# Last output projections tile by tile with kept weights and other normalisations, first loads by two queues, and rotations in steps

## The chip, the cores and the metric

The kernel runs on one core of a Trainium2 chip. The metric is the device time of one execution in microseconds (us); lower is better. The engines are named as in the profile: PE does matmuls and transposes, DVE and ACT elementwise work, POOL a few elementwise steps and DMA issues, SP DMA issues.

## The reference, cut to what matters

```python
# x: (1, 512, 2048) float32; layer 0 is attention, layer 1 retention
def attention_mixer(h, w_in, q_gain, k_gain, w_out, cos, sin):
    q, k, v, g = split(h @ w_in)            # 2048 | 512 | 512 | 2048 columns
    q = apply_rope(rms_norm(q, q_gain), cos, sin) * (128 ** -0.5)
    k = apply_rope(rms_norm(k, k_gain), cos, sin)
    o = softmax(q @ k.T) @ v                # 16 heads, 4 kv heads, not causal
    return (o * silu(g)) @ w_out
def retention_mixer(h, w_in, decay_exp, w_out, cos, sin):
    q, k, v, g = split(h @ w_in)            # 2048 | 2048 | 4096 | 4096 columns
    q, k = apply_rope(q, cos, sin), apply_rope(k, cos, sin) * (256 ** -0.5)
    o = head_group_norm(fwd(q, k, v) + bwd(q, k, v))   # 8 heads, two directions
    return (o * silu(g)) @ w_out
x = layer_norm(ALPHA * x + attention_mixer(x, ...), ln_gain[0], ln_bias[0])
x = layer_norm(ALPHA * x + retention_mixer(x, ...), ln_gain[1], ln_bias[1])
```

## The kernel before

All is float32, and the kernel keeps that precision: each factor is split into a rounded part and a remainder, and a product of two matrices is three matmuls into the same PSUM bank (`mm3`, L218 to L222: both rounded parts L220, the weights' remainder L221, the features' remainder L222). The split (`split`, L103) is a cast on ACT (L104) and a subtraction on DVE (L105). Weights come as chunks of 128 x 1024 (512 KB), loaded by `raw_load` on SP's queue (L112) and split into `whi` and `wlo`; the list `order` says which chunk comes when, `next_chunk` splits two chunks ahead (AHEAD) and loads three more ahead (FETCH). `whi` and `wlo` have three buffers each, raw chunks nine; 32 larger buffers (`x4`) hold features, forms of features, row sums and the heads' operands. There are eight PSUM banks.

PE runs its instructions in the order in which the program issues them (`manual_schedule`); the other engines are put in order by the tile scheduler, and each runs its own list strictly in turn. A `Stream` is a generator of matmul work that is pumped by microseconds between other work.

The input projections are `Block`s of two column blocks of 512 each. A block is made in seven products (Strassen's way, so seven where eight would be needed) of four chunks each; the sums of weights that this takes are made by accumulating DMAs on POOL's queue (`onto`, L116) and by DVE, the sums of features ("forms") by DVE at the places that FORMS lists. `evacuate` combines the products, and `deliver_1` or `deliver_2` hands on a row tile of 128 rows of one column block: v and the gate are stored to DRAM, q and k are first rotated. `turn_soon` puts a rotation off by one to six chunks and then issues it as a whole: `rotate` (attention: square on ACT L528, gain L529, sums L533, six rotation steps L537 to L539, then a power on POOL L414; keys are also scaled L570) or `rope_2` (retention). Three chunks later `put` transposes the result (L431) and stores it.

The attention layer is then computed in four groups, the retention in eight heads, each pumping the output projection of the group or head before it (`Plain`, eight chunks, four column blocks by four row tiles). The last projection of either layer (`out_proj_last`) has no group or head behind it: it goes through all eight chunks for row tiles 0 and 1 and then a second time, loaded and split again, for tiles 2 and 3; after each sum DVE takes its statistics (L402).

After attention `norm_1` normalises two tiles and `turn_1` transposes them into the features of the retention, in pieces of 128 columns, while PE goes on with the second pass and then with the retention's input projection. After retention `norm_2` normalises two tiles at a time: centring and finishing on DVE (L926, L931) for two or three of the four column blocks, the others on ACT (L939) and POOL (L940, L941), and stores them on SP (L922).

At the start, `start` loads the first chunk in two halves and the first features in four pieces, all on SP's queue, then whole chunks.

## Time and profile before

| | us |
|---|---|
| median of 3 runs | 2203.59 (2201.79 to 2204.91) |
| profiled execution, its own time | 2198.51 |
| its span | 2196.6 |
| PE busy in the span | 2142.0 |
| DVE busy | 1586.9 |
| ACT busy | 1043.4 |
| POOL busy | 341.5 |
| mean clock granted to PE | 0.992 of full speed |

The profiled execution is 5.1 us below the median of the runs, and 1.9 us of it lie outside the span. A row of a timeline gives the start, the duration, engine, line, operation and tiles, and in brackets how long the engine had been idle and what it waited for. Matmuls are pipelined, so their durations overlap, and the pace is read from start to start. A granted clock below 1.00 in a window means that PE ran slowly there.

### The profile page before, as it was taken

How to read it: one execution, taken by the hardware profiler on the slowest of the kernel's cores; microseconds unless marked ns; L12 is line 12 of the kernel's file. 1: busy time of each engine (PE TensorE's matmuls, PEld its weight loads, DVE VectorE, ACT ScalarE, POOL GpSimd, SP SyncE). 2: the span in 40 equal slices, each digit the busy share in tenths (PEclk: the TensorE clock that was granted, in tenths of full speed). 3: DMA queues.
4: the chain of work that ended last, by engine and by line, in shares of the span. 5: the costliest groups of instructions: out<-in, count | busy, mean ns of one | idle time of the engine just before them, and what ended most of it. 6: DMA issues, size and time to landing. Idle time of an engine off the chain costs nothing.

```text
span 2196.6 us, 26556 instructions
## 1 busy us (share of the span) xinstructions
PE 2142.0 (98%) x9888; PEld 1767.6 (80%) x9888; DVE 1586.9 (72%) x2189; ACT 1043.4 (48%) x1365; POOL 341.5 (16%) x391
## 2 busy tenths in 40 slices
PE   8999999999999999999999999999999999999994
PEld 6778788888888778878888888888888888888883
DVE  6766978887778986767786676657677666666668
ACT  5545446754455654444444444444465333333332
POOL 0322434000000121211212111111111000000004
PEclk9999999999999999999999999999999999999997
DMA  9976666543215688686777558566667433343342
GB/s 337 211 195 133 169 173 148 184 177 106 95 60 171 207 189 220 163 244 177 176 198 210 132 142 213 155 130 183 178 162 262 160 117 107 122 135 125 101 139 77
DMA packets 111600, 361.42 MB, mean 165 GB/s; under 512 B 13680, under 2 KB 17008, under 8 KB 111472
## 3 DMA queue, kind: packets, MB, share of 16 engines
q1 hardware_dynamic: 76272, 235.99, 32.4%
q0 software_dynamic: 35200, 123.75, 25.7%
q8 instruction: 77, 1.26, 0.2%
q14 instruction: 51, 0.42, 0.1%
HBM read 311.45 MB, written 48.23 MB: 164 GB/s over the span
## 4 chain that ended last, share of the span: by engine, by line
PE 82%; DVE 7%; DMA 4%; issue 3%; POOL 2%; ACT 1%; SPq 0%; POOLq 0%; ACTq 0%; DVEq 0%
PE acc L221 23%; PE acc L222 23%; PE acc L220 23%; PE tr L431 3%; DVE wlo L105 3%; DMA raw<-in_wa_in_dram 2%; PE o L220 2%; PE o L222 2%; PE o L221 2%; DMA raw<-in_wr_in_dram 2%; PE s L220 1%; PE s L222 1%; PE s L221 1%; ACT whi L104 1%; DVE f L105 1%
## 5 line engine op out<-in xcount | busy, mean ns | idle before, releaser
L105 DVE TENSOR_TENSOR wlo<-raw,whi 128x1024 fp32r<-128x1024 f32 (+1 forms) x589 | 716.9, 1221 | 362.2 <-ACT whi L104 355.4
L104 ACT CAST whi<-raw 128x1024 fp32r<-128x1024 f32 (+1 forms) x589 | 618.8, 1052 | 744.2 <-PE acc L222 651.4
L220 PE MATMUL acc<-whi,f 128*128 128x512 f32 x1904 | 750.5, 394 | 9.3 <-ACT f L104 4.5
L221 PE MATMUL acc<-wlo,f 128*128 128x512 f32 x1904 | 745.0, 391 | 6.6 <-DVE wlo L105 6.4
L222 PE MATMUL acc<-whi,f 128*128 128x512 f32 x1904 | 743.8, 391 | 0.7 <-DVE f L105 0.7
L221 PEld LDWEIGHTS acc<-wlo,f 128*128 128x128 f32 x1904 | 358.7, 188 | 85.3 <-DVE wlo L105 13.4
L220 PEld LDWEIGHTS acc<-whi,f 128*128 128x128 f32 x1904 | 358.6, 188 | 83.9 <-ACT whi L104 5.2
L222 PEld LDWEIGHTS acc<-whi,f 128*128 128x128 f32 x1904 | 358.3, 188 | 76.7 <-DVE f L105 1.6
L221 PE MATMUL acc<-wlo,ogh 128*128 128x512 f32 x768 | 301.3, 392 | 11.5 <-DVE wlo L105 11.5
L220 PE MATMUL acc<-whi,ogh 128*128 128x512 f32 x768 | 306.0, 398 | 0.5 <-ACT p L604 0.5
L222 PE MATMUL acc<-whi,ogl 128*128 128x512 f32 x768 | 301.0, 392 | 0.0
L221 PEld LDWEIGHTS acc<-wlo,ogh 128*128 128x128 f32 x768 | 145.5, 189 | 40.5 <-DVE wlo L105 12.7
L222 PEld LDWEIGHTS acc<-whi,ogl 128*128 128x128 f32 x768 | 145.2, 189 | 31.1
L220 PEld LDWEIGHTS acc<-whi,ogh 128*128 128x128 f32 x768 | 145.1, 189 | 28.7 <-ACT p L604 0.9
L116 POOL DMA_DIRECT2D raw<-in_wr_in_dram x104 | 91.7, 882 | 384.0 <-DVE wlo L105 246.7
L365 DVE TENSOR_TENSOR y<-acc,y 128x512 f32<-128x512 f32 x176 | 115.6, 684 | 18.7 <-PE acc L222 18.7
L414 POOL TENSOR_TENSOR rstd<-rs_e,neg_half 128x1 f32<-128x1 f32 x40 | 23.8, 597 | 674.4 <-DVE rs_e L413 674.4
L154 DVE TENSOR_TENSOR raw<-raw,raw 128x1024 f32<-128x1024 f32 x52 | 63.5, 1223 | 35.9 <-DMA raw<-in_wr_in_dram 30.9
L152 DVE TENSOR_TENSOR raw<-raw,raw 128x1024 f32<-128x1024 f32 x68 | 82.1, 1218 | 0.8
L328 ACT COPY t<-acc 128x512 f32<-128x512 f32 x102 | 59.0, 587 | 41.9 <-PE acc L222 38.0
L867 ACT ACTIVATE o<-o,nmr,rstd 128x512 f32<-128x512 f32 x32 | 24.9, 779 | 93.4 <-DVE nmr L425 93.4
L604 ACT ACTIVATE p<-s,nmax,q_rs 128x512 f32<-128x512 f32 x64 | 50.0, 781 | 30.6 <-DVE nmax L602 28.2
(159 smaller groups left out, 2098.8 us busy)
## 6 DMA issues: line engine op xcount, KB each, us to landing
raw<-in_wr_in_dram SPq DMA_DIRECT2D x152, 512.0 KB, 4.8
raw<-in_wr_in_dram POOLq DMA_DIRECT2D x104, 512.0 KB, 6.1
raw<-in_wr_o_dram SPq DMA_DIRECT2D x72, 512.0 KB, 3.5
raw<-in_wa_in_dram SPq DMA_DIRECT2D x67, 512.0 KB, 5.1
raw<-in_wa_in_dram POOLq DMA_DIRECT2D x48, 512.0 KB, 6.4
raw<-in_wa_o_dram SPq DMA_DIRECT2D x40, 512.0 KB, 3.5
qkD<-qkT POOLq DMA_DIRECT2D x32, 256.0 KB, 4.4
vDr<-t POOLq DMA_DIRECT2D x32, 256.0 KB, 5.4
```

The costliest lines, as they stand in the source:

```text
L104: nc.scalar.copy(hi, src)
L105: nc.vector.tensor_sub(lo, src, hi.bitcast(F32))
L116: nc.gpsimd.dma_start(out=x, in_=src, accum_op=ALU.add)
L152: nc.vector.tensor_add(v, v, g[3, c])
L154: nc.vector.tensor_add(v, v, g[2, c])
L220: nc.tensor.matmul(ps, sh, mh, start=start, stop=False, skip_group_check=go_on)
L221: nc.tensor.matmul(ps, sh, ml, start=False, stop=False, skip_group_check=go_on)
L222: nc.tensor.matmul(ps, sl, mh, start=False, stop=stop, skip_group_check=go_on)
L328: nc.scalar.copy(keep[p, t], bk[CHAIN[p]][t])
L365: nc.vector.tensor_add(y, ps, y)
L431: nc.tensor.transpose(out=b[:, tcols(i)], in_=src[:, tcols(i)], identity=ident)
L604: nc.scalar.activation(pt, sb, AF.Exp, scale=rs, bias=nmax, accum_out=self.sm[:, h:h + 1])
```

## The change

It has five parts. (1) `out_proj_last` works tile by tile with kept weights: chunks of a `Plain` from column block `keep` on are split into `x4` buffers (`wkh`, `wkl`) and stay. The attention's last projection does column blocks 0 and 1 for all tiles as before (A_KEEP = 2) and then blocks 2 and 3 for one tile after the other; the retention's keeps all (R_KEEP = 0). The second pass over the chunks goes. (2) The norms are made per tile. `norm_1` keeps DVE's statistics. `norm_2` has its sums from the adding instruction itself (`accum_out`), its squares from ACT, and centres and finishes on DVE alone; `turn_1` takes two tiles together in pieces of 256. (3) `start` loads the first two chunks in halves on SP's queue and the first features on ACT's, and splits both chunks by halves. (4) Attention's column blocks are paired so that each block has one to rotate, and rotations are generators of which one step runs per chunk. (5) The forms 3, 7 and 4 are made in this order over the products 5, 3 and 7, and form 7 overwrites x11.

```diff
-A_COLS = ((("v", 0), ("g", 0)), (("g", 1), ("k", 0)), (("q", 0), ("q", 1)), (("q", 2), ("g", 2)), (("q", 3), ("g", 3)))
+A_COLS = ((("v", 0), ("k", 0)),) + tuple((("g", i), ("q", i)) for i in range(4))
...
+A_KEEP, R_KEEP = 2, 0
...
+            self.w, self.got, self.keep = w, {}, keep
...
-        hi, lo = [wp.tile([P, CH], F32R, tag=n, name=nm(n)) for n in ("whi", "wlo")]
+        if isinstance(blk, Plain) and p >= blk.keep:
+            hi, lo = x4("wkh"), x4("wkl")
+        else:
+            hi, lo = [wp.tile([P, CH], F32R, tag=n, name=nm(n)) for n in ("whi", "wlo")]
...
             elif n == 7:
-                nc.vector.scalar_tensor_tensor(out=x22, in0=x11, scalar=-1.0, in1=x22,
+                nc.vector.scalar_tensor_tensor(out=x11, in0=x11, scalar=-1.0, in1=x22,
                                                op0=ALU.mult, op1=ALU.subtract)
-            split(*self.new_form(n, i), {1: x11, 2: x12, 5: x21, 6: x11, 4: x22, 3: x12, 7: x22}[n])
+            split(*self.new_form(n, i), {1: x11, 2: x12, 5: x21, 6: x11, 4: x22, 3: x12, 7: x11}[n])
...
+        while steps:
+            if next(steps[0], steps) is not steps:
+                break
+            steps.pop(0)
...
-        soon((1, 4, 3, 6)[t], fn, src)
+        steps.append(gen(t, src))
...
+            if last and t not in self.st:
+                self.st[t] = small("ln_st", 24)
+            if last and t not in self.quick:
+                nc.vector.scalar_tensor_tensor(out=y, in0=y, scalar=scale, in1=ps, op0=ALU.mult, op1=ALU.add,
+                                               accum_out=self.st[t][:, c:c + 1])
...
+            if last and t in self.quick:
+                nc.vector.bn_stats(self.st[t][:, 6 * c:6 * c + 6], y)
+        def out_proj(self, og, scale, cols=(0, 1, 2, 3), last=False):
...
+            for c in cols:
...
+                    self.add(t, c, banks[t], scale, last)
+        def mean_rstd(self, t):
+            if t in self.quick:
+                return mean_rstd(self.st[t])
+            mu, neg, sq, rstd = small("k_rs", 4)[:, 0:1], small("nmr"), small("sm", 4), small("rstd")
+            nc.vector.tensor_reduce(out=mu, in_=self.st[t][:, :4], axis=AX.X, op=ALU.add)
+            nc.vector.tensor_scalar_mul(neg, mu, -1.0 / D)
+            nc.vector.tensor_scalar_mul(mu, mu, 1.0 / D)
+            for c in range(4):
+                nc.scalar.activation(temp("sq"), self.y[t, c], AF.Square, bias=neg, accum_out=sq[:, c:c + 1])
+            nc.vector.tensor_reduce(out=neg, in_=sq, axis=AX.X, op=ALU.add)
+            rsqrt(rstd, neg, 1.0 / D, LN_EPS)
+            return mu, rstd
...
+        def out_proj_last(self, og, keep):
+            yield from self.out_proj(og, 1.0, range(keep), True)
+            ws = {}
+            for t in range(NT):
+                for c in range(keep, 4):
+                    b = bank()
+                    for k in range(4):
+                        if t == 0 and k % 2 == 0:
+                            ws[c, k // 2] = next_chunk()
+                        mm3(b, og(k, t), ws[c, k // 2][k % 2], k == 0, k == 3)
+                        yield MM3
+                    self.add(t, c, b, 1.0, True)
+                self.rows.append(t)
...
+    a_out = [Plain(a["wa_o"][g], A_KEEP if g == GROUPS - 1 else 4) for g in range(GROUPS)]
+    r_out = [Plain(a["wr_o"][h], R_KEEP if h == R_HEADS - 1 else 4) for h in range(R_HEADS)]
...
-        outs[-1].add(1)
...
-    FORMS = (((1, 2, 1), (6, 0)), ((1, 2, 3), (6, 1)), ((0, 5, 0), (4, 0)), ((0, 5, 1), (4, 1)),
-             ((0, 5, 2), (3, 0)), ((0, 5, 3), (3, 1)), ((0, 6, 0), (7, 0)), ((0, 6, 1), (7, 1)))
+    FORMS = (((1, 2, 1), (6, 0)), ((1, 2, 3), (6, 1)), ((0, 5, 1), (3, 0)), ((0, 5, 3), (3, 1)),
+             ((0, 3, 0), (7, 0)), ((0, 3, 2), (7, 1)), ((0, 7, 0), (4, 0)), ((0, 7, 2), (4, 1)))
...
+        nc.scalar.copy(small("nmax"), neg_half[:, 0:1])
+        features(0, slice(1, 2))
+        features(0, slice(2, 4))
+        features(1, slice(0, 4))
+        chunks = []
+        for c in range(2):
+            raw = rp.tile([P, CH], F32, tag="raw", name=nm("raw"))
+            for j in range(2):
+                nc.sync.dma_start(out=half(raw, j), in_=half(blk.quarter(11, c), j))
+                if c == j == 0:
+                    features(0, slice(0, 1), nc.sync)
+            chunks.append([raw] + [wp.tile([P, CH], F32R, tag=n, name=nm(n)) for n in ("whi", "wlo")])
+        fetched[0] = 2
         fetch_to(4)
+        for c, (raw, hi, lo) in enumerate(chunks):
+            for j in range(2):
+                k = 2 * c + j
+                if k < 3:
+                    split_features(0, slice(k, k + 1) if k < 2 else slice(2, 4))
+                split(half(hi, j), half(lo, j), half(raw, j))
+            ready.append([(half(hi, j), half(lo, j)) for j in range(2)])
+        split_features(1, slice(0, 2))
+        split_features(1, slice(2, 4))
...
-    def rotate(t, qk, src):
...
+    def rotate(t, qk, src, g, put):
...
+        yield
         ss = small("r_ss", 4)
         nc.vector.tensor_reduce(out=ss, in_=v4(sq), axis=AX.X, op=ALU.add)
+        if qk == 0:
+            rs = q_rs[:, g, t]
+        else:
+            rs = small("k_rs", 4)
+        rsqrt(rs, ss, 1.0 / P, RMS_EPS)
+        yield
+        dst = temp("r_dst")
...
         for i in range(2):
             nc.vector.tensor_tensor(out=tv[:, :, :, i], in0=xv[:, :, :, 1 - i], in1=sb, op=ALU.mult)
+            if i:
+                yield
             nc.vector.tensor_tensor(out=dv[:, :, :, i], in0=xv[:, :, :, i], in1=cb, op=ALU.mult)
+            if not i:
+                yield
             nc.vector.tensor_tensor(out=dv[:, :, :, i], in0=dv[:, :, :, i], in1=tv[:, :, :, i],
                                     op=ALU.subtract if i == 0 else ALU.add)
-        return dst, ss
+        yield
+        if qk:
+            nc.vector.tensor_tensor(out=v4(dst), in0=v4(dst), in1=rs.unsqueeze(2).broadcast_to([P, 4, P]), op=ALU.mult)
+        soon(3, put, dst)
 
...
-                soon(3, put, m)
-            turn_soon(turn, t, src, own)
+            turn_soon(lambda t, src: rotate(t, 0 if kind == "q" else 1, src, g, put), t, src, own)
...
-    total = Sum()
+    total = Sum(range(NT))
...
-    def turn_1(t, c):
...
+    def turn_1(r, m):
+        b = bank("tr")
+        kh, i = m // 4, m // 2 % 2
+        for k in (2 * m, 2 * m + 1):
+            for t in range(2):
+                nc.tensor.transpose(out=b[:, tcols(k % 2 * 2 + t)],
+                                    in_=total.y[2 * r + t, k // 4][:, tcols(k % 4)], identity=ident)
+        for k in (2 * m, 2 * m + 1):
+            o = 256 * (k % 2)
+            f = x2.quarter(r, kh, i)[:, k % 4]
+            if k % 2:
+                nc.vector.tensor_scalar(f, b[:, o:o + 256], lnt[:, 0, k:k + 1], lnt[:, 1, k:k + 1],
+                                        op0=ALU.mult, op1=ALU.add)
             else:
...
+                nc.scalar.activation(f, b[:, o:o + 256], AF.Identity, scale=lnt[:, 0, k:k + 1], bias=lnt[:, 1, k:k + 1])
+        if r == 0 and m % 2:
+            x2.form(1 + kh, i)
...
+            yield
...
+        soon(3, put, m1)
...
-            turn_soon(lambda src: soon(3, put, rope_2(t, src)), t, src, own)
...
     def norm_2(t):
-        mu, rstd = mean_rstd(total.st[t])
...
+        mu, rstd = total.mean_rstd(t)
+        z = [half(m, j) for m in (x4("z", F32), x4("z", F32)) for j in range(2)] if t > 1 else [temp("z") for _ in range(4)]
+        for c in range(4):
...
+            nc.vector.scalar_tensor_tensor(out=z[c], in0=y, scalar=mu, in1=lnp[0][c], op0=ALU.subtract, op1=ALU.mult)
+        for c in range(4):
             y = total.y[t, c]
...
+            nc.vector.scalar_tensor_tensor(out=y, in0=z[c], scalar=rstd, in1=lnp[1][c], op0=ALU.mult, op1=ALU.add)
+            nc.sync.dma_start(out=out[t, :, c * 512:c * 512 + 512], in_=y)
...
-    work = Stream(total.out_proj_last(groups[-1].out), in_stream(r_in, x2, ev2, 1))
...
+    work = Stream(total.out_proj_last(groups[-1].out, A_KEEP), in_stream(r_in, x2, ev2, 1))
+    for r in range(2):
+        for t in (2 * r, 2 * r + 1):
+            work.until(lambda: t in total.rows)
+            norm_1(t)
+        work.pump(13.0 if r else 5.0)
+        for m in (0, 1, 4, 5, 2, 3, 6, 7) if r else range(8):
+            turn_1(r, m)
+            work.pump(2.2 if r else 0.8)
+            if r and m in (5, 7):
+                x2.form(5, m // 2 % 2)
...
-    work = Stream(total.out_proj_last(heads[-1].out))
-    work.pump(20.0)
+    work = Stream(total.out_proj_last(heads[-1].out, R_KEEP))
+    work.pump(5.0)
     ln_params()
...
+    for t in range(NT):
+        work.until(lambda: t in total.rows)
+        norm_2(t)
```

At the end, DVE's rows between the norms of tiles 0 and 1 (`nmr`, L926, L931) and the sums of tiles 2 and 3 in the kernel before; `wlo` are remainders of weights, `y` the row sums:

```order
L926 SCALAR_TENSOR_TENSOR y_13876<-y_13876,mv_17556,ln_gain_17506 128x512
L931 SCALAR_TENSOR_TENSOR y_13872<-y_13872,rstd_17536,ln_bias_17510 128x512
L425 TENSOR_SCALAR nmr_17563<-mv_17556,rstd_17558 128x1
L931 SCALAR_TENSOR_TENSOR y_13876<-y_13876,rstd_17558,ln_bias_17510 128x512
L926 SCALAR_TENSOR_TENSOR y_13876<-y_13876,mv_17556,ln_gain_17506 128x512
L105 TENSOR_TENSOR wlo_17591<-raw_17474,whi_17590 128x1024
L931 SCALAR_TENSOR_TENSOR y_13876<-y_13876,rstd_17558,ln_bias_17510 128x512
L365 TENSOR_TENSOR y_13880<-acc_17530,y_13880 128x512
L365 TENSOR_TENSOR y_13884<-acc_17578,y_13884 128x512
L402 BN_STATS ln_st_17607<-y_13880 128x6
```

and in the changed kernel DVE's rows up to the first step of the first norm (L978); `wkl` are the kept remainders, `ln_st` the sums that the adds give, and six of the eight `wkl` stand in the rows above these:

```order
L106 TENSOR_TENSOR wkl_17317<-raw_17269,wkh_17316 128x1024
L379 SCALAR_TENSOR_TENSOR y_13782,ln_st_17281<-y_13782,acc_17256 128x512
L106 TENSOR_TENSOR wkl_17327<-raw_17284,wkh_17326 128x1024
L379 SCALAR_TENSOR_TENSOR y_13782,ln_st_17281<-y_13782,acc_17283 128x512
L379 SCALAR_TENSOR_TENSOR y_13784,ln_st_17281<-y_13784,acc_17315 128x512
L379 SCALAR_TENSOR_TENSOR y_13784,ln_st_17281<-y_13784,acc_17337 128x512
L410 TENSOR_REDUCE k_rs_17355<-ln_st_17281 128x1
L411 TENSOR_SCALAR nmr_17356<-k_rs_17355 128x1
L412 TENSOR_SCALAR k_rs_17355<-k_rs_17355 128x1
L379 SCALAR_TENSOR_TENSOR y_13786,ln_st_17399<-y_13786,acc_17351 128x512
L978 SCALAR_TENSOR_TENSOR z_17374<-y_13782,k_rs_17355,ln_gain_17306 128x512
```

The splits of the weights stood between the norms' steps; now all are ahead of the first norm, and one tile's adds (L379) are followed by its norm.

From attention to retention, DVE's rows before, around the chunk at which PE waits 2.83 us (`wlo_6447`); `f` are splits of forms, L748 the turning of rows:

```order
L105 TENSOR_TENSOR f_6380<-xf_6374,f_6379 128x4x128
L748 TENSOR_SCALAR xf_6353<-tr_6429,lnt 128x128 x2
L748 TENSOR_SCALAR xf_6400<-tr_6395,lnt 128x128 x2
L402 BN_STATS ln_st_6333<-y_3756 128x6
L105 TENSOR_TENSOR f_6359<-xf_6353,f_6358 128x4x128
L365 TENSOR_TENSOR y_3760<-acc_6362,y_3760 128x512
L105 TENSOR_TENSOR f_6406<-xf_6400,f_6405 128x4x128
L402 BN_STATS ln_st_6336<-y_3760 128x6
L105 TENSOR_TENSOR wlo_6447<-raw_6300,whi_6446 128x1024
L748 TENSOR_SCALAR xf_6374<-tr_6458,lnt 128x128 x2
L748 TENSOR_SCALAR xf_6400<-tr_6475,lnt 128x128 x2
```

and now around the first chunk of the retention's projection that is split behind the last tile's norm (`wlo_6527`, the fourth chunk of that projection); L386 are statistics, L782 the norm, L800 the turning:

```order
L386 BN_STATS ln_st_6153<-y_3768 128x6
L447 BN_AGGR mv_6504<-ln_st_6153 128x2
L442 TENSOR_SCALAR rs_e_6507<-mv_6504 128x1
L454 TENSOR_SCALAR nmr_6510<-mv_6504,rstd_6506 128x1
L106 TENSOR_TENSOR f_6449<-xf_6435,f_6448 128x1024
L782 TENSOR_SCALAR y_3766<-y_3766,mv_6504,rstd_6506 128x512
L800 TENSOR_SCALAR xf_6460<-tr_6455,lnt 128x256
L800 TENSOR_SCALAR xf_6460<-tr_6476,lnt 128x256
L782 TENSOR_SCALAR y_3766<-y_3766,mv_6504,rstd_6506 128x512
L106 TENSOR_TENSOR wlo_6527<-raw_6256,whi_6526 128x1024
L106 TENSOR_TENSOR f_6484<-xf_6460,f_6483 128x1024
L106 TENSOR_TENSOR wlo_6545<-raw_6268,whi_6544 128x1024
```

There is no split of a weight among the sums of the last tile now; the next one stands behind that tile's statistics and norm (L447 to L782).

At the start, ACT's rows before:

```order
L104 ACT_TABLE_LOAD
L104 CAST whi_96<-raw_95 128x512
L104 CAST f_99<-xf_98 128x256 x2
L104 CAST whi_96<-raw_95 128x512
L104 CAST f_99<-xf_98 128x256 x2
L104 CAST whi_123<-raw_119 128x1024
L104 CAST f_127<-xf_121 128x1024
L104 CAST whi_141<-raw_131 128x1024
L104 CAST whi_165<-raw_133 128x1024
```

and now, with DMA issues of the features among them:

```order
L515 DMA xf_95<-in_xq_dram 128x256
L520 ACT_TABLE_LOAD
L520 COPY nmax_101<-neg_half 128x1
L515 DMA xf_95<-in_xq_dram 128x512
L515 DMA xf_96<-in_xq_dram 128x1024
L105 CAST f_97<-xf_95 128x256
L105 CAST whi_110<-raw_106 128x512
L105 CAST f_97<-xf_95 128x256
L105 CAST whi_110<-raw_106 128x512
L105 CAST f_97<-xf_95 128x512
L105 CAST whi_115<-raw_112 128x512 x2
L105 CAST f_99<-xf_96 128x512 x2
```

ACT issues three loads, loads its table early by a copy of one element, and casts the second chunk (`whi_115`) in two halves, the features' last two pieces as one.

More of the change, by code (lines that the diff above doesn't have):

```diff
@@ L483, in start, with features, split_features @@
         blk = order[0][0]
[L484 to L500 removed]
+        xf, fs = [x1.quarter(0, 0, i) for i in range(2)], [x1.new_form(1, i) for i in range(2)]
+        def features(i, ks, eng=nc.scalar):
+            eng.dma_start(out=xf[i][:, ks], in_=a["xq"][0, 0, i][:, ks])
+        def split_features(i, ks):
+            split(*[m[:, ks] for m in fs[i]], xf[i][:, ks])
+        nc.scalar.copy(small("nmax"), neg_half[:, 0:1])
[11 more added lines that the diff above has]
+        fetched[0] = 2
+        fetch_to(4)
+        for c, (raw, hi, lo) in enumerate(chunks):
[7 more added lines that the diff above has]
+        split_features(1, slice(2, 4))
     def tables():
@@ L579, in load_kv @@
         def load_kv(self):
+            assert all(("k", 0, t) in stored for t in range(NT))
             self.k, self.v = x4("k"), x4("v")
@@ L833, in load_qk @@
         def load_qk(self):
+            assert all((self.h, t) in stored for t in range(NT))
             self.qk = split_load(qkD[self.h])
@@ L918, in norm_2 @@
     def norm_2(t):
-        mu, rstd = mean_rstd(total.st[t])
-        def store(c):
-            nc.sync.dma_start(out=out[t, :, c * 512:c * 512 + 512], in_=total.y[t, c])
-        def centre(c):
+        mu, rstd = total.mean_rstd(t)
+        z = [half(m, j) for m in (x4("z", F32), x4("z", F32)) for j in range(2)] if t > 1 else [temp("z") for _ in range(4)]
+        for c in range(4):
             y = total.y[t, c]
-            return nc.vector.scalar_tensor_tensor(out=y, in0=y, scalar=mu, in1=lnp[0][c],
-                                                  op0=ALU.subtract, op1=ALU.mult)
@@ L929, in finish @@
-        def finish(c):
+            nc.vector.scalar_tensor_tensor(out=z[c], in0=y, scalar=mu, in1=lnp[0][c], op0=ALU.subtract, op1=ALU.mult)
+        for c in range(4):
             y = total.y[t, c]
-            nc.vector.scalar_tensor_tensor(out=y, in0=y, scalar=rstd, in1=lnp[1][c], op0=ALU.mult, op1=ALU.add)
-            store(c)
-        own = 2 if t < NT - 1 else 3
-        centre(0)
-        scale, shift = scale_shift(mu, rstd)
-        for c in range(own, 4):
-            y = total.y[t, c]
-            nc.scalar.activation(y, y, AF.Identity, scale=scale, bias=shift)
-            nc.gpsimd.tensor_mul(y, y, lnp[0][c])
-            nc.gpsimd.tensor_add(y, y, lnp[1][c])
-            store(c)
@@ L943, in norm_2 @@
-        finish(0)
-        for c in range(1, own):
-            tc.keep_in_program_order(centre(c))
-            finish(c)
-    ev2 = spill(deliver_2)
-    work = Stream(total.out_proj_last(groups[-1].out), in_stream(r_in, x2, ev2, 1))
-    work.until(lambda: 0 in total.rows)
-    norm_1(0)
-    norm_1(1)
-    work.pump(4.0)
-    for t in range(2):
-        for c in (0, 1, 2, 3):
-            turn_1(t, c)
-            work.pump(1.2)
-    work.until(lambda: 2 in total.rows)
-    norm_1(2)
-    norm_1(3)
```

112 lines of the change are left out of this document (20 added, 92 removed).

## The prediction

> **What bounds the kernel now.** I read the page first, then the waits of PE stretch by stretch, then the timelines around the longest waits.
>
> ```profile
> PE 2142.0 (98%) x9888; PEld 1767.6 (80%) x9888; DVE 1586.9 (72%) x2189; ACT 1043.4 (48%) x1365; POOL 341.5 (16%) x391
> 0.00:30.00 30.00, 22.49 (x74) 16.46 (x74) 14.74 (x18) 15.59 (x20) 0.20 (x4) 0.89 0.93 356
> 50.00:300.00 250.00, 243.32 (x1085) 198.00 (x1084) 192.15 (x263) 130.18 (x154) 88.07 (x71) 1.00 0.72 171
> 660.00:860.00 200.00, 193.29 (x904) 158.62 (x904) 166.63 (x237) 110.53 (x149) 32.81 (x43) 0.99 0.70 192
> 860.00:1300.00 440.00, 436.85 (x1942) 358.69 (x1941) 306.83 (x354) 203.00 (x228) 77.30 (x108) 1.00 0.72 189
> 2150.00:2197.00 47.00, 18.29 (x70) 14.01 (x68) 37.35 (x45) 8.11 (x10) 24.06 (x17) 0.73 0.24 89
> ```
>
> The first line is the page's busy shares; the others are the windows view: the stretch, its length, then busy time of PE, weight loads, DVE, ACT and POOL, the granted clock, DMA share, GB/s. PE is busy for 2142 of 2196.6 us, and both kernels issue the same matmuls and transposes. So the change can only take back the 55 us in which PE is not busy, and stretches at a low clock, and nothing in the middle of a stage at full pace. The idle time lies at five places: 7.5 us in the first 30, 6.7 between 50 and 300 (attention's in-projection), 6.7 between 660 and 860 (attention's last projection and the step to retention), 3.2 up to 1300 (retention's in-projection), and 28.7 in the last 47. The changed parts lie at the same five places.
>
> **The end: the last output projection and the last norms.** PE first, then DVE and POOL.
>
> ```profile
> 2151.68 0.39 PE L222 MATMUL acc<-whi,ogl 128*128 128x512 f32 x1
> 2151.91 0.39 PE L220 MATMUL acc<-whi,ogh 128*128 128x512 f32 x1
> 2160.78 0.80 PE L221 MATMUL acc<-wlo,ogh 128*128 128x512 f32 x1 [8.48 <-DVE wlo L105]
> 2165.18 0.40 PE L222 MATMUL acc<-whi,ogl 128*128 128x512 f32 x1
> ...
> 2176.55 0.39 PE L222 MATMUL acc<-whi,ogl 128*128 128x512 f32 x1
> 2158.44 2.28 DVE L105 TENSOR_TENSOR wlo<-raw,whi 128x1024 fp32r<-128x1024 f32 x1
> 2181.82 1.69 DVE L926 SCALAR_TENSOR_TENSOR y<-y,mv,ln_gain 128x512 f32<-128x512 f32 x1
> 2192.63 0.75 DVE L931 SCALAR_TENSOR_TENSOR y<-y,rstd,ln_bias 128x512 f32<-128x512 f32 x1
> 2181.45 1.52 POOL L940 TENSOR_TENSOR y<-y,ln_gain 128x512 f32<-128x512 f32 x1 [1.17 <-ACT y L939]
> ```
>
> Matmuls follow each other by 0.23 us (2151.68 to 2151.91). The next one comes 8.87 us later, so 8.6 are lost: its small half of the weights (`wlo`, 2158.44) stands on DVE behind the norms of rows 0 and 1. After the wait ten matmuls take 4.40 us (2160.78 to 2165.18) in place of 2.3; that is another 2.1. In the changed kernel each of the eight chunks is split once and kept for all four row tiles, and DVE's order has all eight splits ahead of the first `L978`, the first large step of a norm. The wait then has no cause: **−10.7**. The cover is the previous head's work on PE, beside which the loads and splits now lie; if a kept tile came free late, part of the 8.6 would come back.
>
> After the last matmul (2176.55 + 0.39) the span runs on for 19.7 us to 2196.6. Two tiles are normalised there with POOL's help, and beside POOL's tensor work (2181.45) such a step takes 1.69 us on DVE (2181.82), without it 0.75 (2192.63). After the change POOL has no such work, and only one tile is left:
>
> ```profile
> L528 ACT ACTIVATE r_sq<-t 128x512 f32<-128x512 f32 x14 | 8.8, 630 | 1.5 <-DVE t L339 1.5
> L604 ACT ACTIVATION_READ_ACCUMULATOR p<-s,nmax,q_rs 128x1 f32 x64 | 12.5, 195 | 0.0
> L363 DVE SCALAR_TENSOR_TENSOR y<-y,acc 128x512 f32<-128x512 f32 x16 | 10.6, 680 | 2.4 <-PE acc L222 2.4
> 2179.29 0.99 POOL L414 TENSOR_TENSOR rstd<-rs_e,neg_half 128x1 f32<-128x1 f32 x1 [15.75 <-DVE rs_e L413]
> 2178.77 0.38 DVE L418 BATCH_NORM_AGGREGATE mv<-ln_st 128x2 f32<-128x24 f32 x2
> 2179.07 0.14 DVE L413 TENSOR_SCALAR rs_e<-mv 128x1 f32<-128x1 f32 x1
> ```
>
> The last add takes 0.68; the sum of four numbers and two scalings 0.2 + 2 x 0.14 = 0.5; four squares on ACT with their accumulator reads 4 x (0.63 + 0.20) = 3.3, which hide DVE's four centring steps (4 x 0.75 = 3.0); a small sum and a scaling 0.3; POOL's power 0.99 with about 0.4 to be noticed; four finishing steps 4 x 0.75 = 3.0; and, as now, 3.2 from the end of the last of them (2193.38) to the end of the span for its store. Together 12.4, so **−7.3**. An add that also sums is not in the trace. Its nearest row is the plain one, 0.68; the ACT pair suggests up to 0.2 more, and if it were a second pass, 1.4. I take 0.68, since only the last add is on the path: −6.6 to −8.5 (the latter if the small steps overlap). DVE keeps up before that: a tile gives PE 16 x 3 matmuls x 0.227 = 10.9 us, and DVE 4 x 0.68 + 8 x 0.75 and a microsecond of small work, 9.7.
>
> **From attention to retention.** Again PE, then DVE, then one row of PE's waits from 660 to 860 us (its columns: us in total, times, the longest).
>
> ```profile
> 716.88 0.39 PE L220 MATMUL acc<-whi,ogh 128*128 128x512 f32 x1
> 720.09 0.50 PE L221 MATMUL acc<-wlo,ogh 128*128 128x512 f32 x1 [2.83 <-DVE wlo L105]
> 721.43 0.63 PE L220 MATMUL acc<-whi,ogh 128*128 128x512 f32 x1
> ...
> 724.42 0.53 PE L221 MATMUL acc<-wlo,ogh 128*128 128x512 f32 x1
> 718.23 0.69 DVE L402 BATCH_NORM_STATS2 ln_st<-y 128x6 f32<-128x512 f32 x1
> 718.83 1.21 DVE L105 TENSOR_TENSOR wlo<-raw,whi 128x1024 fp32r<-128x1024 f32 x1
> PE acc L221 <- DVE wlo L105: 4.6, 2, 2.8
> ```
>
> PE's idle time in this stretch is 6.7 us, 4.6 of it for `wlo`; the seven matmuls from 721.43 to 724.42 take 2.99 in place of 1.6 and cost 1.4 more. The late split (718.83) stands on DVE behind sums of the row tiles and the forms made of the first rows. Now no chunk is split a second time, which takes eight splits of 1.21 us from DVE over the stage, the rows' turning goes in pieces of 256 columns, and the forms are split in one piece of 1024 in place of two of 512. What can be late next is the fourth chunk of the retention's projection: on DVE it stands behind the norm of the last tile. That chain is 0.68 + 0.68 + 0.38 + 0.14 + 0.99 + 1.0 and some turning and splitting, about 7.5 us, against three chunks of PE work, 3 x 2.72 = 8.2. It just fits. I take **−7**, between −2 (the wait comes back there) and −8.
>
> **The start.** PE, then ACT.
>
> ```profile
> 8.88 0.40 PE L222 MATMUL acc<-whi,f 128*128 128x512 f32 x1
> 11.40 0.79 PE L220 MATMUL acc<-whi,f 128*128 128x512 f32 x1 [2.13 <-ACT whi L104]
> 17.95 0.49 PE L221 MATMUL acc<-wlo,f 128*128 128x512 f32 x1
> 10.31 1.04 ACT L104 CAST whi<-raw 128x1024 fp32r<-128x1024 f32 x1 [0.89 <-DMA raw<-in_wa_in_dram]
> 11.59 1.05 ACT L104 CAST f<-xf 128x1024 fp32r<-128x1024 f32 x1 [0.24 <-DMA xf<-in_xq_dram]
> ```
>
> The second chunk lands at 10.3; PE waits 2.1 us for its cast, and then runs slowly until 17.95. Cast by halves, the chunk's first half is ready about half a cast sooner, and the loads are issued earlier. But two loads of 512 KB each land 1.28 us apart (10.31 and 11.59, where ACT was waiting for them), so the third chunk cannot be split much before it is now, at about 15; PE starts it at 17 now. The bound on the gain is therefore 2 to 4, and nothing is gained if the features, now on a second queue, land ahead of the second chunk. I take **−2.5**, from 0 to −4.
>
> The rows show the clock low after a wait of 2.13 us and after one of 2.83. The Trainium skill ("TensorE: Matmul & The Clock Gate", Part 1) says that the half rate comes after an idle window of about 3.4 us; the two rows do not agree with a full window of idling, and the measurement decides. By that rule a short wait left at the start would cost no clock, and the start would give −4, the sum 2168.5; by the rows it may, and I stay at −2.5.
>
> **Rotations in steps, and the order of the forms.** PE's waits from 50 to 300 us, the first three rows; then POOL's powers.
>
> ```profile
> PE tr L431 <- DVE r_dst L539: 2.0, 4, 1.1
> PE acc L220 <- DVE t L335: 1.5, 2, 1.3
> PE tr L431 <- DVE r_dst L570: 1.4, 1, 1.4
> L414 POOL TENSOR_TENSOR q_rs<-rs_e,neg_half 128x4 f32<-128x4 f32 x16 | 52.8, 3300 | 67.1 <-DVE rs_e L413 67.1
> ```
>
> Of the 6.4 us in this stretch 4.9 come from rotated columns that were late, or from a batch of rotation that stood ahead of an eviction. One step per chunk and a transpose three chunks after the last step take these away. The same twenty rotations remain, so DVE's sum is unchanged. I take **−4** (0 to −6.4). In retention's in-projection 3.0 us of waits remain, most for `wlo` behind such batches: **−2** (0 to −3). The order of the forms moves additions and splits of 1.2 us between chunks; it goes into these two bounds.
>
> **Sum.** −10.7 − 7.3 − 7 − 2.5 − 4 − 2 = −33.5. The profiled execution took 2198.5 us (span 2196.6 and 1.9 around it) and would take 2165.0; the median of the runs is 5.1 above it. On the median: **2170 us**, 1.5% less.
>
> **Rivals.**
> The queues (15%). By the landing rows a second queue brings no byte sooner, and the features may delay the second chunk; the start then gives nothing: 2172.5. The Trainium skill ("DMA: Bandwidth & Descriptors", Issuing engines are not separate DMA queues) has this as a rule: several issuing engines save only the time to issue. The trace agrees so far: 1.28 us from landing to landing, with issues long done.
>
> The late split at the transition (13%). If the fourth chunk's split comes more than 0.7 us later than I count, PE waits and the clock falls as at 720: 5 of the 7 are lost, 2175. For it speaks that DVE is busy 166.6 of 200 us there.
>
> The end stall returns (9%). The kept splits need buffers which the last head's tiles hold; if half wait for them, as one split did for 8.5 us, the 10.7 are gone: 2181. Against it: the order puts them beside the last head's evictions.
>
> Nothing happens (3%): each wait taken away is replaced by one as long, 2203.
>
> Slower (5%): POOL's queue. POOL adds the second weight quarters by DMA and also computes the powers, 3.30 us each. A step per chunk puts a power between each two of these additions. An addition has four chunks, 10.9 us, and lands in 6.4 (median of the page's table of issues), so one power fits and two don't: 2 x 3.3 − 4.5 = 2.1 us of PE time. Over twenty rotations that is 42 us: 2212. It decides from 1.7 us each. Against it: now a block with two query columns has eight powers, and PE's waits in that stretch show none on a DMA.
>
> ```profile
> raw<-in_wa_in_dram POOLq DMA_DIRECT2D x48, 512.0 KB, 6.4
> ```
>
> **Numbers.** My forecast has 55%, with 2163 to 2177 as its own range. The terms' ends: all at their best −10.7 − 8.5 − 8 − 4 − 6.4 − 3 = −41 (2163); all at their worst, with the end stall gone, −10.7 − 6.6 − 2 = −19 (2184). For eight in ten I go 4 us below the best sum, since a matmul lost at a low clock counts in no wait, and up to the end stall's return: **2159 to 2182**. That leaves out the last two rivals, 8%, and some of each edge. Faster by more than 0.2% (about what a measurement of this kernel can tell from no change) has 55 + 15 + 13 + 9 = 92%, the same 3%, slower 5%.
>
> **What would show it.** In the profile after: no PE wait for a kept split in the last 60 us; from the last matmul to the span's end some 12 us; PE idle under 2 us at the transition; no wait on `r_dst` up to 300 us; the second chunk's first matmul before 11 us. I am wrong if PE waits on weights landing by POOL's queue, or if the span after the last matmul stays above 16 us.

## The result, and the profile after

| | before | after |
|---|---|---|
| median of the runs, us | 2204.11 (2201.79 to 2204.91, 4 runs) | 2171.57 (2169.36 to 2173.45, 4 runs) |
| profiled execution's own time, us | 2198.51 | 2169.95 |
| its span, us | 2196.6 | 2168.2 |

The ratio is 0.9857, with a 95% interval from 0.9845 to 0.987: 1.4% faster. The forecast was 2170 us, range 2159 to 2182. By the profiled executions the gain is 28.6 us, by the medians 32.5; the profiled one of before lay 5.6 us below its median, that of after 1.6.

The page of after, its busy shares, then its windows (the same stretches as before, the last one moved to the new end):

```profile
PE 2134.7 (98%) x9888; PEld 1765.1 (81%) x9888; DVE 1562.1 (72%) x2176; ACT 1021.5 (47%) x1346; POOL 311.0 (14%) x377
0.00:30.00 30.00, 23.71 (x97) 19.23 (x98) 19.16 (x23) 17.46 (x23) 0.20 (x4) 1.00 0.94 369
50.00:300.00 250.00, 243.15 (x1077) 197.96 (x1076) 190.86 (x261) 128.75 (x152) 83.13 (x71) 0.99 0.71 171
660.00:860.00 200.00, 196.59 (x920) 161.34 (x919) 156.88 (x209) 100.31 (x120) 34.30 (x46) 1.00 0.65 177
860.00:1300.00 440.00, 437.07 (x1946) 359.25 (x1945) 312.49 (x357) 204.71 (x230) 75.43 (x106) 1.00 0.69 186
2125.00:2169.00 44.00, 31.90 (x141) 26.09 (x139) 32.11 (x76) 11.74 (x32) 2.92 (x4) 0.90 0.26 96
```

PE runs 97 matmuls in the first 30 us where it ran 74, and idles 3.4 us at the transition in place of 6.7. But between 50 and 300 us it idles as long as before (6.9 us), and up to 1300 almost so.

A wait and the low clock behind it are best counted together. For that I sum, over PE's rows, the distance from one start to the next beyond the pace at full clock (0.227 us for 512 columns, 0.119 for 256, 0.108 for a transpose into `tr`). This lost pace, by stretches of the profiled execution, with the start of the first matmul and the tail from the end of the last matmul to the end of the span:

| kernel | first | to 50 | 50 to 110 | 110 to 300 | 300 to 660 | 660 to 860 | 860 to 1300 | from 2100 | tail |
|---|---|---|---|---|---|---|---|---|---|
| before | 4.6 | 9.2 | 2.4 | 7.7 | 6.6 | 11.3 | 6.5 | 11.4 | 19.7 |
| after | 6.3 | 1.8 | 10.6 | 1.4 | 7.3 | 6.4 | 5.9 | 0.1 | 11.3 |

The columns' differences, rounded as here, sum to −28.3 us; the spans differ by 28.4. The end gives 11.3 + 8.4 of it. The start gives 5.7 up to 50 us, and 8.2 go again between 50 and 110: at 110 us the changed kernel has lost 18.7 us in all, that of before 16.2.

The end of after, first two rows by tile (how often, the shortest, median and longest in ns, then the first and the last start in us), then DVE's timeline behind the last matmul:

```profile
L106 DVE TENSOR_TENSOR wkl<-raw,wkh x8: 1212/1217/1220, 2103.1 to 2116.8; 128x1024 fp32r<-128x1024 f32 x8
L978 DVE SCALAR_TENSOR_TENSOR z<-y,k_rs,ln_gain x16: 742/745/752, 2127.6 to 2160.2; 128x512 f32<-128x512 f32 x16
```

```profile
2156.93 0.69 DVE L379 SCALAR_TENSOR_TENSOR y<-y,acc 128x512 f32<-128x512 f32 x1 [1.31 <-PE acc L227]
2157.55 0.08 DVE L379 DVE_READ_ACCUMULATOR y<-y,acc 128x1 f32 x1
2157.67 0.16 DVE L410 TENSOR_REDUCE k_rs<-ln_st 128x1 f32<-128x4 f32 x1
...
2158.24 2.74 DVE L978 SCALAR_TENSOR_TENSOR z<-y,k_rs,ln_gain 128x512 f32<-128x512 f32 x4
2161.01 0.16 DVE L415 TENSOR_REDUCE nmr<-sm 128x1 f32<-128x4 f32 x1
2161.20 0.15 DVE L442 TENSOR_SCALAR rs_e<-nmr 128x1 f32<-128x1 f32 x1
2162.08 2.74 DVE L981 SCALAR_TENSOR_TENSOR y<-z,rstd,ln_bias 128x512 f32<-128x512 f32 x4 [0.72 <-POOL rstd L443]
```

All eight kept splits start before the first large step of a norm, and the list of PE's waits is empty from 2100 us on. The add that also sums takes 0.69 us and 0.08 for the read, so the sum is nearly free here. The chain is the one forecast: add, squares on ACT beside the centring, power, four finishing steps (2.74 together), store. And PE's waits from 50 to 110 us, after, with the row of ACT's casts that waited for loads:

```profile
PE acc L226 <- DVE wlo L106: 3.4, 6, 0.8
PE acc L225 <- DVE t L348: 1.9, 1, 1.9
PE acc L225 <- ACT whi L105: 1.0, 1, 1.0
ACT whi L105 <- DMA raw<-in_wa_in_dram: 11.7, 6, 2.8
```

Before, PE had one wait of 1.3 us for `wlo` there and one of 0.2, and the casts waited 3.8 us for loads.

### The profile page after: what moved, and what is told of

Same layout as the page of the kernel before. It is cut to its first block, busy times and chain, and to the rows that moved or that the text cites. A ratio compares the mean times of both kernels' runs of the same rounds, so it can differ in the third digit from the quotient of the medians.

```text
span 2168.2 us, 26411 instructions
## 1 busy us (share of the span) xinstructions
PE 2134.7 (98%) x9888; PEld 1765.1 (81%) x9888; DVE 1562.1 (72%) x2176; ACT 1021.5 (47%) x1346; POOL 311.0 (14%) x377
## 4 chain that ended last, share of the span: by engine, by line
PE 85%; DMA 6%; DVE 4%; issue 2%; POOL 1%; ACT 1%; SPq 0%; POOLq 0%; DVEq 0%; ACTq 0%
PE acc L226 24%; PE acc L227 24%; PE acc L225 24%; DMA raw<-in_wa_in_dram 4%; PE tr L460 3%; PE o L225 2%; PE o L227 2%; DVE wlo L106 2%; PE o L226 2%; DMA raw<-in_wr_in_dram 2%; PE s L227 1%; PE s L225 1%; PE s L226 1%; ACT whi L105 1%; POOL q_rs L443 1%
## 5 line engine op out<-in xcount | busy, mean ns | idle before, releaser
L106 DVE TENSOR_TENSOR wlo<-raw,whi 128x1024 fp32r<-128x1024 f32 (+1 forms) x562 | 683.2, 1218 | 349.4 <-ACT whi L105 346.7
L105 ACT CAST whi<-raw 128x1024 fp32r<-128x1024 f32 (+1 forms) x562 | 588.9, 1050 | 688.2 <-PE acc L227 619.3
L225 PE MATMUL acc<-whi,ogh 128*128 128x512 f32 x672 | 266.4, 396 | 0.4 <-ACT ogh L105 0.4
L227 PE MATMUL acc<-whi,ogl 128*128 128x512 f32 x672 | 262.4, 391 | 0.0
L226 PE MATMUL acc<-wlo,ogh 128*128 128x512 f32 x672 | 262.0, 390 | 0.0
L227 PEld LDWEIGHTS acc<-whi,ogl 128*128 128x128 f32 x672 | 126.1, 188 | 27.4 <-DVE ogl L106 0.4
L225 PEld LDWEIGHTS acc<-whi,ogh 128*128 128x128 f32 x672 | 126.3, 188 | 24.8 <-ACT ogh L105 0.8
L226 PEld LDWEIGHTS acc<-wlo,ogh 128*128 128x128 f32 x672 | 126.4, 188 | 24.1
L384 DVE TENSOR_TENSOR y<-acc,y 128x512 f32<-128x512 f32 x160 | 105.7, 685 | 17.6 <-PE acc L227 17.6
```

Source lines behind the costliest of these rows:

```text
L105: nc.scalar.copy(hi, src)
L106: nc.vector.tensor_sub(lo, src, hi.bitcast(F32))
L225: nc.tensor.matmul(ps, sh, mh, start=start, stop=False, skip_group_check=go_on)
L226: nc.tensor.matmul(ps, sh, ml, start=False, stop=False, skip_group_check=go_on)
L227: nc.tensor.matmul(ps, sl, mh, start=False, stop=stop, skip_group_check=go_on)
L384: nc.vector.tensor_add(y, ps, y)
```

## The experiments

My theory was the account above: the end is worth 19 to 20 us, the transition about 5, the rotations in steps about 6, and the start nothing, since the loads set the pace up to 110 us. The rivals are in the expectations. All times below are medians, with the ratio to the kernel before, measured beside it. The line numbers in a run's rows are those of its own kernel, and its trace is one execution.

### One part undone at a time

**The start.** `start` as before.

```diff
-        nc.scalar.copy(small("nmax"), neg_half[:, 0:1])
-        features(0, slice(1, 2))
...
+        fetched[0] = 1
+        fetch_to(2)
+        load_quarter(0, 0, 1)
+        make_chunk()
```

> The changed kernel with the old start (all first loads on SP's queue, only the first chunk in halves). Theory A, the landings of the weights set the pace of the first 110 us whatever the start does: the time stays within 2.5 us of the changed kernel (2169 to 2174), PE loses 5 us or more again before 50 us and waits at least 4 us less between 50 and 110 us. Rival B, the start is worth what it gained by 50 us and the waits at 50 to 110 us come from elsewhere: slower by 4 to 6 us (2175 to 2178), and the waits at 50 to 110 us stay at about 9 us.

2172.08 us, ratio 0.986 (0.9847 to 0.9873), against 0.9857 of the changed kernel. Undoing the start costs nothing that can be measured. Lost pace up to 50 us is 7.6 with the first matmul at 4.6 (12.2 together, in place of 8.1), and 5.2 in place of 10.6 between 50 and 110. That is theory A, though PE's waits alone, without the low clock, are 2.8 us fewer, not 4. Its waits from 50 to 110 us:

```profile
PE acc L225 <- DVE t L348: 2.0, 1, 2.0
PE acc L226 <- DVE wlo L106: 1.5, 2, 0.8
ACT whi L105 <- DMA raw<-in_wa_in_dram: 9.9, 6, 2.5
```

The landings say why. The third chunk landed at 10.4 us in the changed kernel and at 12.4 with the old start. But the accumulating loads behind them landed at 49.0, 52.8, 56.6 and 60.1 us in the one and at 48.9, 53.4, 57.1 and 60.9 in the other, some 3.8 us apart where PE takes 2.7 per chunk, and the one that a cast waited for at 93 us landed at 93.3 and 93.1. The lead in loading was spent by then.

**The rotations as a whole**, pairing as changed; and then **the old pairing too**.

```diff
-        steps.append(gen(t, src))
+        soon((1, 4, 3, 6)[t], lambda: [None for _ in gen(t, src)])
```

```diff
-A_COLS = ((("v", 0), ("k", 0)),) + tuple((("g", i), ("q", i)) for i in range(4))
+A_COLS = ((("v", 0), ("g", 0)), (("g", 1), ("k", 0)), (("q", 0), ("q", 1)), (("q", 2), ("g", 2)), (("q", 3), ("g", 3)))
```

> The changed kernel with each rotation issued as a whole again, one to six chunks after its column is done, the pairing of columns and the order of forms as changed. Theory A, the steps are what took the rotations' waits away (6.4 us between 110 and 300 us): slower by 3 to 6 us (2175 to 2178), with PE waits on a rotation's result or on an eviction behind one. Rival B, it was the pairing with one column to rotate per block: within 1.5 us (2170 to 2173).

> The changed kernel with the old pairing of columns and each rotation as a whole, so all of the fourth part undone. Theory A (steps): about as the one with whole rotations and the new pairing, within 1.5 us of it. Rival B (pairing): 3 us or more slower than that one, since two blocks have no rotation and one has eight.

Whole rotations with the new pairing: 2187.11 us, 0.9923 (0.9909 to 0.9937). With the old pairing too: 2176.01 us, 0.9874 (0.9861 to 0.9887). The six runs of the first lie from 2179.8 to 2189.7, wider than those of any other kernel here, so its size is rough. The first went the way of theory A, by far more than it said, and the second went the other way than either said: with whole rotations the new pairing is 11 us worse than the old one. The fourth part as a whole is worth about 4 us, with intervals that overlap slightly. The edit puts the rotations of both layers back. In the profile of the first, rotation waits are back, behind larger ones for splits:

```profile
PE tr L460 <- DVE r_dst L597: 3.1, 3, 1.4
PE tr L460 <- DVE r_dst L593: 2.1, 2, 1.3
PE tr L460 <- ACT p L654: 1.9, 1, 1.9
```

The third row lies at 411 us, in the attention's first group, where the last block's column is still being rotated. Lost pace grows by 4.0 us from 110 to 300, 3.8 from 300 to 660, 2.1 in each of the next two stretches. That is 12 of the 13.7 us between the profiled executions; the medians lie 15.5 apart. With the old pairing too, lost pace is 6.3 us more than in the changed kernel from 110 to 300 us and 2.2 less from 50 to 110.

**The places of the forms** as before.

```diff
-    FORMS = (((1, 2, 1), (6, 0)), ((1, 2, 3), (6, 1)), ((0, 5, 1), (3, 0)), ((0, 5, 3), (3, 1)),
-             ((0, 3, 0), (7, 0)), ((0, 3, 2), (7, 1)), ((0, 7, 0), (4, 0)), ((0, 7, 2), (4, 1)))
+    FORMS = (((1, 2, 1), (6, 0)), ((1, 2, 3), (6, 1)), ((0, 5, 0), (4, 0)), ((0, 5, 1), (4, 1)),
+             ((0, 5, 2), (3, 0)), ((0, 5, 3), (3, 1)), ((0, 6, 0), (7, 0)), ((0, 6, 1), (7, 1)))
```

> The changed kernel with the old places of the forms (4, then 3, then 7 over the products 5 and 6). Theory A, the waits between 50 and 110 us come from loads, and the forms are worth nothing: within 1.5 us (2170 to 2173). Rival B, the new order crowds DVE at the products 5 to 7 and makes some of these waits: faster by 2 to 4 us (2168 to 2169). Rival C, the new order takes a wait away: slower by 2 us or more.

2174.84 us, 0.987 (0.9857 to 0.9882): about 3 us slower, as rival C has it, but with intervals that overlap, so the time alone does not show it. The trace does: the loss is not between 50 and 110 us (11.2) but at the transition, 10.3 in place of 6.4, where the retention's forms are made.

**The retention's end**, two passes and old norms; and **the old norm alone**, per tile, on kept weights.

```diff
-A_KEEP, R_KEEP = 2, 0
+A_KEEP, R_KEEP = 2, 4
...
+        if outs is r_out:
+            outs[-1].add(1)
...
-    for t in range(NT):
-        work.until(lambda: t in total.rows)
-        norm_2(t)
+    work.until(lambda: 0 in total.rows)
+    norm_2(0)
+    norm_2(1)
+    work.drain()
+    norm_2(2)
+    norm_2(3)
```

```diff
-    total = Sum()
+    total = Sum(range(NT))
...
-        mu, rstd = total.mean_rstd(t)
+        mu, rstd = mean_rstd(total.st[t])
...
+            nc.scalar.activation(y, y, AF.Identity, scale=scale, bias=shift)
+            nc.gpsimd.tensor_mul(y, y, lnp[0][c])
+            nc.gpsimd.tensor_add(y, y, lnp[1][c])
```

> The changed kernel with the old end of the retention: two passes over the last projection's chunks and the old norms by DVE, ACT and POOL. Theory A, the terms of the end add up: slower by 18 to 21 us (2190 to 2193): the wait of about 8.5 us for a weight's remainder behind the norms and 2 us of low clock come back, and the span after the last matmul is 19 to 20 us again. Rival B, something else had shortened the end (the loads, the state of the clock): slower by less than 12 us.

> The changed kernel with kept weights tile by tile, but the old statistics and the old norm (parts of it on ACT and POOL) for each tile. Theory A, keeping the weights alone takes the end stall away, and one tile's norm in place of two alone shortens the tail: no PE wait in the last 60 us, and the span after the last matmul is about 14 us: 2 to 4 us slower than the changed kernel (2173 to 2176). Rival B, the norm by POOL slows DVE beside it so far that tile 3's adds are late: 6 us or more slower.

Two passes: 2190.39 us beside 2201.81 of before, 0.995 (0.9935 to 0.9965), so 20 us slower than the changed kernel by the ratios. The wait is back to the hundredth:

```profile
2153.32 0.80 PE L226 MATMUL acc<-wlo,ogh 128*128 128x512 f32 x1 [8.48 <-DVE wlo L106]
```

and so are the lost pace (11.3) and the tail (19.6). The old norm on kept weights: 2174.12 us, 0.9871 (0.9856 to 0.9886), about 3 us slower by the ratios, with intervals that overlap, no PE wait at the end and a tail of 12.1. Of the end's 19.7 us, nearly all comes from keeping the weights and going tile by tile; the new norm has 0.8 of it in the trace, and more than that is not shown.

**The attention's end**, two passes, norms by pairs, pieces of 128.

```diff
-A_KEEP, R_KEEP = 2, 0
+A_KEEP, R_KEEP = 4, 0
...
-            turn_1(r, m)
-            work.pump(2.2 if r else 0.8)
+            turn_1(t, c)
+            work.pump(1.2)
```

> The changed kernel with the old end of the attention: two passes over the last projection, norms by pairs, features turned in pieces of 128 columns. Theory A, this part is worth what the trace shows from 660 to 860 us: slower by 4 to 7 us (2175 to 2179), with a PE wait of 2 to 3 us for a weight's remainder there. Rival B, the gain there comes from the other order of the forms and the steps: slower by less than 2 us.

2172.27 us, 0.9867 (0.9853 to 0.9882): 2 us slower by the ratios, with overlapping intervals. The wait of 2.8 us for `wlo` and one of 1.2 for a row sum return at 712 and 728 us, and others, at 785, do not come: lost pace there 8.5 in place of 6.4. Traces of one and the same code differ by 1.6 us in this stretch (6.3 or 7.9; the last section has the reason), so the 2 us of the tile-by-tile form are not clear of that; the 3.9 us of the forms' places (10.3 with the old ones) are, and they are the larger part of the 4.9 gained. Theory A's wait came, but not its time; rival B's number is nearer.

### Are the waits from 50 to 110 us waits for loads?

The products 1 and 2 need one load per chunk, the product 5 of the first blocks two. Three blocks' products 1 and 2 ahead give the loads more time.

```diff
-    a_in = [Block(a["wa_in"][g], g < 2) for g in range(A_G)]
+    a_in = [Block(a["wa_in"][g], g < 3) for g in range(A_G)]
...
-        for b in ins[:2]:
+        nf = 3 if ins is a_in else 2
+        for b in ins[:nf]:
             b.add((1, 2))
```

> The changed kernel with the products 1 and 2 of three of the attention's blocks ahead of the other five products, in place of two blocks; that loads 2 MB more in all, but later. Theory A, the waits between 50 and 110 us come from weights that land too late while the DMA engines are full: the third block's 8 chunks need one load each, so the loads catch up; the 10.6 us lost there fall to 4 or less, and the time falls by 4 to 7 us (2164 to 2168). Rival B, they come from DVE's work in these products (forms, sums, first rotations): they stay, only later, and the time is within 2 us.

2176.22 us beside 2201.81, 0.9883 (0.9867 to 0.99): slower, and neither. The small waits from 54 to 65 us are gone, but PE stands 8.8 us at 74 us. What DVE did there:

```profile
67.67 1.22 DVE L106 TENSOR_TENSOR wlo<-raw,whi 128x1024 fp32r<-128x1024 f32 x1
75.04 0.17 DVE L753 TENSOR_SCALAR de<-de 128x16 f32<-128x16 f32 x1 [6.15 <-DMA de<-in_decay_dram]
```

The preparation of the retention's decays depends on one small load alone, so the scheduler puts it early; DVE runs in order and waits 6.2 us for a small load behind large ones. In the changed kernel the same preparation has a power on POOL at 80 us, ahead of accumulating loads for which ACT then waits:

```profile
80.72 4.29 POOL L752 TENSOR_TENSOR xg<-two,de 128x16 f32<-128x16 f32 x1
83.63 3.19 POOL L117 DMA_DIRECT2D raw<-in_wa_in_dram  x2
93.35 1.04 ACT L105 CAST whi<-raw 128x1024 fp32r<-128x1024 f32 x1 [2.40 <-DMA raw<-in_wa_in_dram]
```

So the next kernels tie it to the last rotation's result (zero times that plus two), which changes no value.

```diff
-    nc.vector.memset(two, 2.0)
-    nc.vector.tensor_scalar_mul(de, de, -1.0)
+    nc.vector.tensor_scalar(two, q_rs[:, GROUPS - 1].rearrange("p t h -> p (t h)"), 0.0, 2.0, op0=ALU.mult, op1=ALU.add)
+    nc.vector.scalar_tensor_tensor(out=de, in0=de, scalar=-0.5, in1=two, op0=ALU.mult, op1=ALU.mult)
```

> The changed kernel with the preparation of the decays (sixteen small steps, a power on POOL of 4.3 us and a table load on ACT at 80 to 112 us) made to depend on the last rotation, so that it comes some 290 us later; computed values are the same. Theory A, this preparation stands on POOL ahead of accumulating weight loads and on DVE and ACT ahead of splits, and makes part of the waits between 90 and 106 us: these fall by 2 to 5 us (2167 to 2170). Rival B, the accumulating loads are late by themselves: within 1.5 us (2170 to 2173).

> Three blocks' products 1 and 2 ahead, and the preparation of the decays late. In the kernel with three blocks the small waits at 54 to 65 us went, and one wait of 8.8 us came at 74 us, where DVE stood 6.2 us for the load of the decay exponents. Theory A, without that the loads have caught up: at most 3 us lost between 50 and 110 us, 2163 to 2168. Rival B, the loads are late there in any case: the wait only takes another name, 2171 or more.

Alone: 2171.38 us, 0.9855 (0.9842 to 0.9868), no change; lost pace from 50 to 110 us stays at 10.4. With three blocks: **2166.0 us, 0.9829 (0.9816 to 0.9843)**, faster than both kernels. Its lost pace from 50 to 110 us is 0.6, and the one row of waits there:

```profile
PE acc L225 <- DVE t L352: 0.4, 1, 0.4
```

The casts that waited 11.7 us for loads in this stretch wait for none now, and the lost pace does not come later instead (it grows by some 1.5 us from 110 to 300), so the waits were for loads. Once these had time, they went; the preparation mattered only with three blocks ahead. One of the waits has a second part: that of 1.95 us at 104 us was for an eviction on DVE, which from 97.9 us on worked without a pause through splits whose chunks had landed late and steps of a rotation. Why the changed kernel stands 2.5 us further back at 110 us than the kernel before is open: with the old start 17.4 us are lost by then, with the fourth part undone 17.2, so neither has it alone.

Two more on the start, in this better kernel: the first features ahead of the table load on ACT's queue, and the old start.

```diff
+        features(0, slice(0, 1))
         nc.scalar.copy(small("nmax"), neg_half[:, 0:1])
         features(0, slice(1, 2))
...
-                if c == j == 0:
-                    features(0, slice(0, 1), nc.sync)
```

> As the kernel before it in this list, with the first piece of the features ahead on ACT's queue, its other pieces behind the table load. Theory A, the first matmul came 1.7 us later than before the change since seven loads shared the DMA engines: it now comes at 5.3 us or earlier, and where no wait for loads follows the time falls by 0.5 to 1.5 us more. Rival B, the lead is used up by waits for the second and third chunk: within 0.5 us of that kernel.

> Three blocks ahead and the decays late, with the old start. Theory A, the new start's lead of 4 us at 50 us is worth nothing in the changed kernel only since the loads are late up to 110 us; here they are not late, so the old start costs its 4 us: 2169 to 2171.5, and PE loses under 2 us between 50 and 110 us. Rival B, the lead is paid back to the loads here too: within 1.5 us of the kernel with the new start (2164.5 to 2167.5).

The swap: 2167.75 us, 0.9839 (0.9826 to 0.9853), not faster; the first matmul came at 6.1, not by 5.3, and waits of 0.5 and 0.8 us for a chunk's two parts followed at 14.4 and 15.6 us. The old start: 2169.82 us, 0.9849 (0.9835 to 0.9862), 3.8 us slower than with the new start. By its time this is theory A. Its trace shows only half: lost pace with the first matmul is 10.6 to 50 us in place of 9.8, then 1.7 in place of 0.6, and 1.6 more lie at the transition, where kernels with one and the same code differ by as much (6.3 or 7.9). So where loads are not late the start is worth between 2 us (the trace) and 4 (the times), and nothing that can be measured in the changed kernel.

## Why the prediction was right, and where it was not

- **The end stall, −10.7.** Right: 11.3, shown by the part undone. The mechanism was as stated; all kept splits ran ahead of the norms.
- **The tail, 12.4 us, −7.3.** Right in its chain; mis-sized by 1.1. The last tail is 11.3: POOL's power takes 0.54 us in place of 0.99 and 0.2 to be noticed in place of 0.4, the four squares 2.9 in place of 3.3, and four finishing steps 2.74 in place of 3.0.
- **From attention to retention, −7.** Measured −4.9, with PE idle for 3.4 us where I had named under 2 as the sign. I counted on the old waits to go and named the fourth chunk's split as what comes next; the waits that are left lie at 785 us, at the 23rd chunk, behind the retention's forms and first rotations. The forms' places, which I had put at nothing with a bound of a chunk's split, are worth 3.9 us there by the trace.
- **The start, −2.5.** This step failed. I priced it by its own 18 us, bounded by landings of 1.28 us per 512 KB, and let the gain stand to the end. The bound did not hold: the third chunk landed at 10.4 in place of 12.8 us, and the two queues had issued by 2.6 us what SP's alone had issued by 4.0. So the lead was larger than forecast up to 50 us (5.7), and then went: PE came earlier to chunks whose loads came no earlier. The first matmul came later (6.3 against 4.6): the first weights landed at 4.5 in place of 3.6 us and the first features at 5.3 in place of 3.9, with six loads issued in the first 1.7 us in place of three. That these loads held each other up is argued, not isolated by a run. The rival of the queues, which I gave 15%, was the case for the start, but not for its reason, as bytes did come sooner: its 2172.5 is 1 us from the median.
- **The clock.** I left open whether a short wait costs clock. It can, and not by its length alone: see the last section.
- **Rotations in steps, −4.** With the part undone as a whole the time rises by about 4 us, the size forecast, and no wait on `r_dst` is left up to 300 us. The table's −6.3 from 110 to 300 us is the larger side of that. What I missed is that the pairing alone would have cost: undone singly, the steps are worth some 15 us.
- **Retention's in-projection, −2.** Measured −0.6. This step failed too: I had the waits for `wlo` behind rotations, and they stay with rotations in steps. The longest left, 1.57 us at 1176, is for a split behind a sum of weights on DVE, and that sum had waited 2.72 us for a load.
- **POOL's queue (slower, 5%).** The kernel is not slower. But the sign I named for it came between 50 and 110 us: casts that PE waited for began as loads of POOL's queue landed (52.8, 56.6 and 93.3 us). None of these loads had a rotation's power ahead of it, as the first of those starts at 91.2 us; what stood ahead of weight loads was the decays' power, and moving it away alone changed nothing.

In the profiled executions the gain is 28.4 us where I had 33.5, so the sum was 5 us too large. That the median came within 1.6 us of the forecast is luck: I added the 5.1 us between profiled execution and median of the kernel before, and after the change the two lie 1.6 us apart. The sign and the bulk rest on the end, which the experiments show: 19.7 us where I had 18.0. The other terms came to −8.6 where I had −15.5.

## What to carry to other kernels

A stall at the very end has nothing behind it that can take the gain back, so it is worth its full size; a lead won at the start is worth only what the loads behind it allow, so add up bytes until PE has caught up with them. Small preparations that depend on little can be put into the busiest stage by the scheduler and stop an engine that runs its list in order, here for 6.2 us; tie them to a late result. Here, reordering so that the loads have time (one load per chunk first), with the preparation out of the way, took 5.6 us off the changed kernel, in which the faster start was worth nothing.
